# Layer boundary of a two-layer streaming encoder step: the second normalisation from three sums gathered in the projection, six channel units over k-tiles, adaLN block 6 between them, and the first adaLN loads behind a gate

## The chip, the core and the metric

One core of a Trainium2 chip runs the whole program in one launch. The metric is device time of an execution in microseconds (us): the median of the runs, and beside it one execution taken with the hardware profiler, whose span is read below. The engines are called by their names in the profile: PE (TensorE, matmuls; PEld are its weight loads), DVE (VectorE), ACT (ScalarE), POOL (GpSimd) and SP (SyncE, which issues most loads).

## What is computed

320 tokens (256 of a prompt, 64 of a sample) of width 2048 pass two layers. Layer 0 mixes a state-space part and sliding-window attention, layer 1 is a gated short convolution. Around each mixer stands the same frame, and the change lies where the frame of layer 0 ends and that of layer 1 begins:

```python
def rms_norm(x, w):
    y = x * lax.rsqrt(jnp.mean(x * x, axis=-1, keepdims=True) + EPS)
    return y * w
def modulate(x, c, w_ada, b_ada, g_pre):
    mod = jax.nn.silu(c) @ w_ada + b_ada             # adaLN
    shift, scale, gate = jnp.split(mod[:, None, :], 3, axis=-1)
    return rms_norm(x, g_pre) * (1 + scale) + shift, gate
for layer in range(DEPTH):                           # 2 layers, prompt and sample alike
    h, gate = modulate(x, c, w_ada[layer], b_ada[layer], norm_pre[layer])
    o = mixer(h)                                     # ends with "@ w_out"; layer 1 begins with "h @ w_in"
    x = x + gate * rms_norm(o, norm_post[layer])
```

So x1 = x + r0 * t, where t is layer 0's output o times its gate and norm weight, and r0 = rsqrt(mean(o^2) + EPS) is one number per token. Layer 1 needs r1 = rsqrt(mean(x1^2) + EPS). Since r0 does not depend on the channel, mean(x1^2) = mean(x^2) + 2 r0 mean(x t) + r0^2 mean(t^2).

## The kernel before

All activations lie transposed in SBUF: 128 channels on the partitions by 320 tokens, 16 such tiles ("n" or "kt", 0 to 15) for the width 2048, four to a buffer of a pool called act. A product takes fp32 weights and activations that are split in two parts each, so that one 128x128 by 128x320 product is three matmuls (high by high, high by low, low by high). `block` loads 1 MB of weights by SP, splits each half of it (`split`: ACT writes the high part of 128x1024, DVE subtracts to get the low part) and queues the half's 24 matmuls; queued halves ("jobs") run two later, and between them `tick` advances side work.

The names that matter here:

- The projection of layer 0 ends in eight calls of `pair` (m = 0 to 7), each for two tiles n of the output. Their PSUM tiles are "pot", the weights' parts "wot". After the last matmul of tile n `close` runs: DVE adds the PSUM to the tile o, ACT squares it (fq), DVE adds the square to facc, ACT multiplies the tile by its gate.
- adaLN comes in blocks of 512 columns; block b's four quarters (`ada_pe`, sub = 0 to 3) are 16 small matmuls each. Quarters of block 5 and the first of block 6 stand between the pairs, seven more (6,1 to 7,3) in the boundary (`more`); their weights "adaw" are loaded by SP. At the same time `ada_side` works block 4 of layer 1 on DVE (adac, two 128x512 products per step of a load "adas"), at a rate per tick.
- The boundary follows: `by_token` sums facc over the partitions (three 128x1 matmuls), `rstd` makes r0 from it on 128x3 elements and spreads it to all partitions by three matmuls (rp0b). `residual` then takes each tile: DVE multiplies o by r0, DVE (even n) or POOL (odd n) adds x and writes x1 (`x<-xr,o`), ACT squares it (x1q), and PE adds the square into x1s by an fp32 matmul with ones. From x1s come r1t, r1 and r1b in the same way, and `modulate` makes layer 1's input, hh and hl, tile by tile.
- Layer 1's first channel block c = 0 has four units n (u, gc, g, gb), worked over k-tiles: `wc_block(j)` for j = 0 to 3 takes k-tiles 4j to 4j+3 for all four units (PSUM tiles "c"), so that PE can start when the first tiles of hh are there. The blocks c = 1 to 31 take one unit after the other over all 16 k-tiles (PSUM tiles "pc").
- At the start of the program `ada_fetch(2)` has POOL issue four loads "adaw" of 512 KB for blocks that PE takes up later, while SP loads x, the adaLN weights w0[0] to w0[7] of the first two tiles ("w" in the profile, PE's "adaf") and the first weights of the mixer ("early", "ahead").

The order of most instructions is decided when the program is built, by a scheduler that goes by its own costs; where `pin[0]` is set, PE and SP keep the order of the code. DVE, ACT and POOL each run their instructions strictly in the order that results.

## Time and profile before

| | us |
|---|---|
| median of 3 runs (lowest, highest) | 2163.41 (2160.16, 2163.43) |
| the profiled execution, whole time | 2157.34 |
| its span, which the views divide | 2155.6 |
| PE busy in the span | 2125.1 (99%) |
| DVE busy | 1403.8 (65%) |
| ACT busy | 898.5 (42%) |
| POOL busy | 188.2 (9%) |

In the profiled execution layer 0's last projection ends at about 980 us, and layer 1's channel blocks run from 1005 us on. Times in the views are microseconds from the start of the span. "start, us" rows give a begin and a duration; "x32" is a count of instructions; "<-" in a name reads "written from"; "[... <-DMA adaw]" is idle time of the engine ahead of the row and what ended it. Matmuls are pipelined, so that one shows about 0.31 us but the next starts 0.15 us after it.

### The profile page before, as it was taken

How to read it: one execution, taken by the hardware profiler on the slowest of the kernel's cores; microseconds unless marked ns; L12 is line 12 of the kernel's file. 1: busy time of each engine (PE TensorE's matmuls, PEld its weight loads, DVE VectorE, ACT ScalarE, POOL GpSimd, SP SyncE). 2: the span in 40 equal slices, each digit the busy share in tenths (PEclk: the TensorE clock that was granted, in tenths of full speed). 3: DMA queues.
4: the chain of work that ended last, by engine and by line, in shares of the span. 5: the costliest groups of instructions: out<-in, count | busy, mean ns of one | idle time of the engine just before them, and what ended most of it. 6: DMA issues, size and time to landing. Idle time of an engine off the chain costs nothing.

```text
span 2155.6 us, 38215 instructions
## 1 busy us (share of the span) xinstructions
PE 2125.1 (99%) x15659; PEld 2065.6 (96%) x15659; DVE 1403.8 (65%) x2273; ACT 898.5 (42%) x1473; POOL 188.2 (9%) x433
## 2 busy tenths in 40 slices
...
GB/s 340 388 287 176 168 161 185 157 262 188 172 184 205 173 181 213 272 267 233 172 176 169 159 176 159 178 172 177 155 164 169 163 163 174 171 137 157 150 145 88
DMA packets 88767, 408.82 MB, mean 190 GB/s; under 512 B 10992, under 2 KB 11920, under 8 KB 52496
## 3 DMA queue, kind: packets, MB, share of 16 engines
...
q8 instruction: 122, 2.00, 0.4%
q14 instruction: 53, 0.43, 0.1%
...
## 4 chain that ended last, share of the span: by engine, by line
PE 58%; DVE 1%; issue 1%; DMA 0%; POOL 0%; ACT 0%; POOLq 0%; ACTq 0%; DVEq 0%
PE pc L47 41%; PE poe L47 5%; PE pod L47 5%; PE pot L47 3%; PE c L47 1%; PE pos L47 1%; PE adap L47 1%; DVE adac L285 1%; PE pb L47 0%; PE x1s L47 0%; DMA adaw<-in_wada 0%; DVE wot0l L174 0%; DVE wos7l L174 0%; DVE o L1173 0%; PE st L47 0%
## 5 line engine op out<-in xcount | busy, mean ns | idle before, releaser
L285 DVE SCALAR_TENSOR_TENSOR adac<-adas,cs,adac 128x512 f32<-128x512 f32 x420 | 300.4, 746 | 60.0 <-DMA adas<-in_wada 60.0
L1241 POOL COPY ncc<-cp 128x2 f32<-128x2 f32 x32 | 6.0, 186 | 940.5 <-DVE cp L1239 940.5
L47 PE MATMUL adap<-adaw,cs 128*32 128x128 f32 x1152 | 37.8, 277 | 2.8 <-DMA adaw<-in_wada 2.7
L956 POOL COPY nca<-xp 128x3 f32<-128x3 f32 x24 | 23.0, 958 | 196.2 <-ACT xp L954 196.2
L47 PEld LDWEIGHTS adap<-adaw,cs 128*32 128x32 f32 x1152 | 30.9, 111 | 7.7 <-issue 4.1
L762 ACT ACTIVATE pr<-s,mx 128x192 f32<-128x192 f32 (+2 forms) x80 | 29.8, 406 | 14.9 <-DVE mx L757 14.9
L1246 DVE SCALAR_TENSOR_TENSOR cc<-cp,ccw,cc 128x322 f32<-128x322 f32 x64 | 35.3, 552 | 1.1
L541 POOL DMA_DIRECT2D adaw<-in_wada x48 | 25.2, 530 | 91.7 <-PE adap L47 48.8
L1239 DVE TENSOR_TENSOR cp<-pc,u 128x256 f32<-128x256 f32 x31 | 13.2, 425 | 30.3 <-PE pc L47 30.2
L990 ACT ACTIVATE sg<-sg,acum 128x128 f32<-128x128 f32 (+1 forms) x96 | 29.3, 376 | 8.4 <-POOL sg L982 8.3
L1254 DVE TENSOR_TENSOR sgg<-pc,sgg 128x320 f32<-128x320 f32 x31 | 15.2, 490 | 19.0 <-PE pc L47 18.9
L961 DVE SCALAR_TENSOR_TENSOR cv<-xp,convaw,cv 128x323 f32<-128x323 f32 x48 | 26.5, 552 | 0.7
L982 POOL TENSOR_SCALAR_AFFINE_SELECT sg<-sg 128x512 f32<-128x512 f32 (+1 forms) x24 | 21.9, 920 | 38.5 <-DMA sg<-acs_b 38.4
L598 DVE TENSOR_TENSOR q<-s,q 128x320 f32<-128x320 f32 x32 | 15.0, 489 | 15.0 <-PE s L47 15.0
L1160 DVE TENSOR_TENSOR oo<-poe,oo 128x320 f32<-128x320 f32 x16 | 7.9, 492 | 25.6 <-PE poe L47 25.6
L47 PE MATMUL s<-hh,ws_0h 128*128 128x320 f32 x64 | 20.2, 315 | 1.2 <-ACT ws_1h L170 1.2
L47 PE MATMUL s<-hl,ws_0h 128*128 128x320 f32 x64 | 19.9, 311 | 1.5 <-DVE hl L493 1.5
L47 PE MATMUL s<-hh,ws_1h 128*128 128x320 f32 x64 | 20.5, 320 | 0.0
L47 PE MATMUL s<-hh,ws_2h 128*128 128x320 f32 x64 | 20.4, 319 | 0.0
L47 PE MATMUL s<-hh,ws_2l 128*128 128x320 f32 x64 | 19.8, 309 | 0.0
L47 PE MATMUL s<-hh,ws_1l 128*128 128x320 f32 x64 | 19.8, 309 | 0.0
L47 PE MATMUL s<-hh,ws_0l 128*128 128x320 f32 x64 | 19.8, 309 | 0.0
...
## 6 DMA issues: line engine op xcount, KB each, us to landing
...
adaw<-in_wada POOLq DMA_DIRECT2D x48, 512.0 KB, 9.5
...
```

The source lines that it names most:

```text
L47: ins = f(*a, **k)
L285: V.scalar_tensor_tensor(acc[s], w, c, acc[s], op0=ALU.mult, op1=ALU.add)
L541: G.dma_start(t[m], i["wada"][q[0], q[1], q[2]][:, 2 * m : 2 * m + 2, :])
L598: V.tensor_tensor(dst, ps, a, op=ALU.add)
L762: S.activation(pr[m][u // 2][:, u % 2, a : a + CH[c][2]], ss[m][u // 2][:, u % 2, a : a + CH[c][2]], AF.Exp, bias=mx[:, j, u : u + 1], sca ...
L956: G.tensor_copy(nca[:, ci, 0, :], xp[:, 256:259])
L961: V.scalar_tensor_tensor(cv, xp[:, n : n + 323], cw[:, ci, n : n + 1], cv, op0=ALU.mult, op1=ALU.add)
L982: G.affine_select(sg, sg, pattern=[[0, 4], [1, nt]], base=0, channel_multiplier=-1, compare_op=ALU.is_ge, fill=NEG)
L990: S.activation(sgs[b][n][:, h, :], sgs[b][n][:, h, :], AF.Exp, bias=acum[0:nt, b, hd : hd + 1])
L1239: V.tensor_tensor(xp[:, 2:258], ps[:, 0:256], u[:, 0:256], op=ALU.mult)
L1246: V.scalar_tensor_tensor(cv, xp[:, m : m + 322], ccw[:, c, m : m + 1], cv, op0=ALU.mult, op1=ALU.add)
L1254: V.tensor_tensor(sg, ps, sg, op=ALU.mult)
```

## The change

Five things are changed at once.

1. In the projection `close` does more for each tile: ACT also squares the gated tile (tq), DVE adds that square to tacc[0], POOL multiplies x by the tile (tx) and adds the product to tacc[1]. The last tile's three squares and products stay apart (last_sq), and its product is DVE's.
2. In the boundary the mean of x1's squares is put together on 128x3 elements from sums over the partitions of facc, tacc[0], tacc[1] (p9) and of the last tile's three (q9), r0, and the saved mean square of x (vxx). `residual`, the 16 squares x1q and the matmuls x1s go. `root` and `spread` are the two halves of `rstd`.
3. The first k-tile stage takes six units, the four of c = 0 and the first two of c = 1, four k-tiles at a time. Its first weights (wj) are loaded and split ahead of the boundary. x1 and hh, hl are made in this stage, tile by tile, x1 three tiles ahead (`x1_tile`, `h_tile`); POOL does 14 of the 16 adds to x1.
4. Block 6's four quarters stand in the boundary, with weights loaded ahead (two by POOL into act buffers, two by SP in eight pieces adaz); block 7's stand in the k-tile stage. Blocks 8 to 11 on DVE begin after c = 1 and no longer before c = 0.
5. At the start the first four adaLN loads of POOL wait for w0[7] to land. POOL also copies vxx there.

The core of the diff (ada_turn's and the removed parts' lines are cut):

```diff
     def rstd(ps, n, name, table=False, base=None):
...
+        if name == "r0":
+            G.tensor_copy(vxx, v)
...
-    ada_fetch(2)
+    landed = wk.tile([128, 1], F32, tag="rt", name="landed")
+    behind = G.tensor_copy(landed, w0[7][:, 3, 0:1])
+    with tc.issue_after(behind.ins):
+        ada_fetch(2)
...
     def close(n, l, ps):
...
         for s, a, b in SEGS:
             S.activation(t[:, a:b], t[:, a:b], AF.Identity, scale=mod[l][:, 2, n, s : s + 1])
+        if l == 0:
+            x = xr[n // 4][:, n % 4, :]
+            if n < KT - 1:
+                sumsq(tacc[0], t, n == 0, f"tq{n}")
+                c = tacc[1] if n == 0 else stile([128, T], f"tx{n}")
+                G.tensor_tensor(c, x, t, op=ALU.mult)
+                if n:
+                    G.tensor_tensor(tacc[1], tacc[1], c, op=ALU.add)
+            else:
+                last_sq.extend([stile([128, T], f"tq{n}"), stile([128, T], f"tx{n}")])
+                S.activation(last_sq[1], t, AF.Square)
+                V.tensor_tensor(last_sq[2], x, t, op=ALU.mult)
...
     for m in range(8):
         pair(i["wos"][1, m], f"ot{m}", ys, 8, ...)
-        if m in (0, 1, 2, 4, 6):
+        if m in (0, 1, 2, 4):
             ada_pe(*later.pop(0), make=mmps, end=True)
+        if m == 5:
+            first += later
+            ada_fetch(2)
     finish_side()
...
+    wj = wp.tile([128, 16, 128], F32, tag="w", name="wj")
+    nc.sync.dma_start(wj, i["wc"][0])
+    ab = [halves(wj[:, 0:8, :], "wja"), halves(wj[:, 8:16, :], "wjb")]
     flush()
+    pin[0] = True
...
+    for m, a in enumerate((facc, tacc[0], tacc[1])):
+        sums9(p9, m, a)
...
+    sums9(q9, 0, last_sq[0])
+    quarter()
+    sums9(q9, 1, last_sq[1])
+    sums9(q9, 2, last_sq[2])
...
+    y0 = root(w9[:, 0:3], "rp0")
+    quarter()
+    pb0 = spread(y0, "rp0")
+    wt, wx = w9[:, 3:6], w9[:, 6:9]
+    V.scalar_tensor_tensor(wt, q9[:, 3:6], 1.0 / D, b9[:, 3:6], op0=ALU.mult, op1=ALU.add)
+    V.scalar_tensor_tensor(wx, q9[:, 6:9], 2.0 / D, b9[:, 6:9], op0=ALU.mult, op1=ALU.add)
+    V.tensor_tensor(wt, wt, y0, op=ALU.mult)
+    V.tensor_tensor(wt, wt, wx, op=ALU.add)
+    V.tensor_tensor(wt, wt, y0, op=ALU.mult)
+    V.tensor_tensor(wt, wt, vxx, op=ALU.add)
+    V.tensor_scalar(wt, wt, EPS, None, op0=ALU.max)
+    y1 = root(wt, "r1")
+    quarter()
+    row6 = ada_row(1, 6, quarter())
+    ada_turn(1, 6, row6)
...
+    def x1_tile(n, rs):
+        t, to, x = ot[n // 4][:, n % 4, :], x1[n // 4][:, n % 4, :], xr[n // 4][:, n % 4, :]
+        V.tensor_tensor(t, t, rs, op=ALU.mult)
+        (V if n < 2 else G).tensor_tensor(to, x, t, op=ALU.add)
+    def h_tile(n, rs):
...
+        V.tensor_tensor(xn, x1[g][:, k, :], rs, op=ALU.mult)
...
+            S.activation(hi, xn[:, c], AF.Identity, scale=sc, bias=sh)
...
+                S.activation(t[:, c], hi.bitcast(F32), AF.Identity, scale=-1.0, bias=sh)
...
+                V.scalar_tensor_tensor(lo, xn[:, c], sc, t[:, c], op0=ALU.mult, op1=ALU.add)
+    x1_tile(0, pb0)
+    S.activation(rs0, pb0, AF.Copy)
+    for n in range(1, 4):
+        x1_tile(n, rs0)
+    pb1 = spread(y1, "r1")
+    h_tile(0, pb1)
+    S.activation(rs1, pb1, AF.Copy)
+    for n in range(1, 4):
+        x1_tile(n + 3, rs0)
+        h_tile(n, rs1)
+    ada_fetch(2)
...
         if c == 0:
+            jobs.append(joint)
+            c1_block(0)
             for j in range(1, 4):
-                wc_block(j)
-                modulate(x1, rs, 1, 4 * j, 4, h1)
+                for m in range(2):
+                    for n in (4 * j + 2 * m, 4 * j + 2 * m + 1):
+                        if n + 3 < KT:
+                            x1_tile(n + 3, rs0)
+                        h_tile(n, rs1)
+                    if m == 0:
+                        wc_block(j)
+                    else:
+                        c1_block(j)
+                    if j == 1:
+                        quarter()
+                        ada_fetch(2)
+                    elif j == 2:
+                        got = quarter()
...
```

The order of instructions at three places follows; the numbers in names are the buffers'. First PE at the boundary. Before, from the last matmul of the projection to the first sums of squares, quarters of adaLN (adap) lie around the sums of facc (rp0t) and the spread of r0 (rp0b):

```order
L47 MATMUL pot_11168<-ysh_10343,wot7l_11097 128x320
L47 MATMUL adap_11027<-adaw_6_1_11218,cs 32x128 x16
L47 MATMUL adap_11027<-adaw_6_2_11240,cs 32x128 x5
L47 MATMUL rp0t<-ones,facc_9502 128x1 x3
L47 MATMUL adap_11027<-adaw_6_2_11240,cs 32x128 x11
L47 MATMUL adap_11027<-adaw_6_3_11258,cs 32x128 x16
L47 MATMUL rp0b<-rp0d,ones 128x128 x2
L47 MATMUL rp0b<-rp0d,ones 128x64
L47 MATMUL adap_11276<-adaw_7_0_11277,cs 32x128 x16
L47 MATMUL x1s<-x1q_11316,ones 128x320
L47 MATMUL x1s<-x1q_11321,ones 128x320
```

Now, on the same engine from the same place, where rp and rq are p9 and q9, and the last of the three rp waits for POOL's sum tacc[1]:

```order
L47 MATMUL pot_11277<-ysh_10347,wot7l_11168 128x320
L47 MATMUL rp_11311<-ones,facc_9506 128x1 x3
L47 MATMUL rp_11311<-ones,tacc_10363 128x1 x3
L47 MATMUL rp_11311<-ones,tacc_10364 128x1 x3
L47 MATMUL rq_11312<-ones,fq_11303 128x1 x3
L47 MATMUL adap_6_11329<-adaw_00_11011,cs 32x128 x8
L47 MATMUL adap_6_11329<-adaw_01_11012,cs 32x128 x8
L47 MATMUL rq_11312<-ones,tq_11307 128x1 x3
L47 MATMUL rq_11312<-ones,tx_11308 128x1 x3
L47 MATMUL adap_6_11329<-adaw_10_11015,cs 32x128 x8
L47 MATMUL adap_6_11329<-adaw_11_11016,cs 32x128 x8
L47 MATMUL rp0b<-rp0d,ones 128x128 x2
```

The sums of squares over 16 tiles are gone from PE, 18 sums of one column stand in their place, and from the last rp on every matmul waits in line behind them. Second DVE in the middle of the projection. Before, between one tile's add of PSUM (L1160) and the second next:

```order
L1160 TENSOR_TENSOR o_5157<-pot_10614,o_5157 128x320
L285 SCALAR_TENSOR_TENSOR adac_4_0_10588<-adas_4_2_10477,cs,adac_4_0_10588 128x512
L385 TENSOR_TENSOR facc_9502<-facc_9502,fq_10644 128x320
L285 SCALAR_TENSOR_TENSOR adac_4_1_10589<-adas_4_2_10477,cs,adac_4_1_10589 128x512
L174 TENSOR_TENSOR wot3l_10674<-wot_10671,wot3h_10673 128x1024
L285 SCALAR_TENSOR_TENSOR adac_4_0_10588<-adas_4_3_10586,cs,adac_4_0_10588 128x512
L285 SCALAR_TENSOR_TENSOR adac_4_1_10589<-adas_4_3_10586,cs,adac_4_1_10589 128x512
L1160 TENSOR_TENSOR o_5439<-pot_10677,o_5439 128x320
L285 SCALAR_TENSOR_TENSOR adac_4_0_10588<-adas_4_4_10627,cs,adac_4_0_10588 128x512
L385 TENSOR_TENSOR facc_9502<-facc_9502,fq_10707 128x320
L174 TENSOR_TENSOR wot3l_10713<-wot_10671,wot3h_10712 128x1024
```

Now, over the same kind of stretch a little later:

```order
L1166 TENSOR_TENSOR o_5443<-pot_10750,o_5443 128x320
L286 SCALAR_TENSOR_TENSOR adac_4_0_10604<-adas_4_5_10677,cs,adac_4_0_10604 128x512
L286 SCALAR_TENSOR_TENSOR adac_4_1_10605<-adas_4_5_10677,cs,adac_4_1_10605 128x512
L175 TENSOR_TENSOR wot4l_10798<-wot_10795,wot4h_10797 128x1024
L388 TENSOR_TENSOR facc_9506<-facc_9506,fq_10780 128x320
L388 TENSOR_TENSOR tacc_10363<-tacc_10363,tq_10785 128x320
L286 SCALAR_TENSOR_TENSOR adac_4_0_10604<-adas_4_6_10718,cs,adac_4_0_10604 128x512
L286 SCALAR_TENSOR_TENSOR adac_4_1_10605<-adas_4_6_10718,cs,adac_4_1_10605 128x512
L1166 TENSOR_TENSOR o_5443<-pot_10801,o_5443 128x320
L175 TENSOR_TENSOR wot4l_10843<-wot_10795,wot4h_10842 128x1024
```

Each tile's group has one add more (tacc), and the adac steps have stayed. Third POOL, before the projection's end. Before, its instructions from the loads of xr on, with no arithmetic until the adds of x1 in the boundary:

```order
L1183 DMA xr_10353<-in_xT 128x1280
L1183 DMA xr_10354<-in_xT 128x1280
L88 DMA ccw<-in_convcw 128x96
L88 DMA cprevc<-in_cprevc 128x64
L1222 TENSOR_TENSOR x_0_11208<-xr_10351,o_5157 128x320 x2
L1222 TENSOR_TENSOR x_1_11209<-xr_10352,o_5439 128x320 x2
```

Now, from the same loads on, the first of 29 operations that run beside the projection:

```order
L1202 DMA xr_10358<-in_xT 128x1280
L544 DMA adaw_00_11011<-in_wada 128x1024
L544 DMA adaw_01_11012<-in_wada 128x1024
L544 DMA adaw_10_11015<-in_wada 128x1024
L1182 TENSOR_TENSOR tacc_10364<-xr_10355,o_5161 128x320
L544 DMA adaw_11_11016<-in_wada 128x1024
L1182 TENSOR_TENSOR tx_10558<-xr_10355,o_5161 128x320
L1184 TENSOR_TENSOR tacc_10364<-tacc_10364,tx_10558 128x320
L1182 TENSOR_TENSOR tx_10629<-xr_10355,o_5161 128x320
L1184 TENSOR_TENSOR tacc_10364<-tacc_10364,tx_10629 128x320
```

POOL has moved from idle to two operations for each tile of the projection.

More of the change, by code (lines that the diff above doesn't have):

```diff
@@ L304, in ada_row, with ada_turn @@
         return row
[L306 to L307 removed]
+    def ada_turn(l, b, row, one=None, pool=None):
+        pt = pool.tile([128, 128], F32, tag="ada", name=f"adat{l}_{b}") if pool else sps([128, 128], f"adat{l}_{b}_{one}")
         if one is None:
@@ new lines, in spread @@
+    def spread(y, name):
+        dg = wk.tile([128, 3, 128], F32, tag="dg", name=name + "d", bufs=1)
+        pb = sps([128, T], name + "b")
+        for b, (t0, c0, n_) in enumerate(TB):
+            V.tensor_scalar(dg[:, b, :], ident, y[:, b : b + 1], None, op0=ALU.mult)
+            PE.matmul(pb[:, t0 + c0 : t0 + c0 + n_], lhsT=ones, rhs=dg[:, b, c0 : c0 + n_], start=True, stop=True)
+        return pb
+    w9 = wk.tile([128, 9], F32, tag="w9", name="w9", bufs=1)
+    V.scalar_tensor_tensor(w9[:, 0:3], q9[:, 0:3], 1.0 / D, b9[:, 0:3], op0=ALU.mult, op1=ALU.add)
@@ L1257, in hybrid_stream_step @@
     h1 = ([], [])
-    p4 = [once(f"c0{n}", mmps if n < 2 else lambda name: sps([128, T], name)) for n in range(4)]
-    def wc_block(j):
-        en = []
-        for n in range(4):
-            en += [(p4[n], 4 * j + k, j == 0 and k == 0, j == 3 and k == 3,
-                    (lambda ps, n=n: channels(0, n, ps)) if j == 3 and k == 3 else None) for k in range(4)]
-        block(i["wc"][j], f"wc{j}", en, h1)
-    pq = mmps("x1s")
-    def square(n, t):
-        sq = stile([128, T], f"x1q{n}")
-        S.activation(sq, t, AF.Square)
-        PE.matmul(pq, lhsT=ones, rhs=sq, start=n == 0, stop=n == KT - 1)
@@ L1274, in more @@
-    def more(n=1):
-        for _ in range(n):
-            if later:
-                ada_pe(*later.pop(0), make=mmps, end=False)
-    more(1)
-    residual(0, xr, square, [V, G] * 8)
-    wc_block(0)
-    row = stile([1, T], "x1row")
-    V.tensor_copy(row, pq[0:1, :])
-    sums = by_token(row, "r1t", ones[0:1, 0:1])
-    more(3)
-    rs = rstd(sums, D, "r1", True)
-    assert not later
-    for b in (6, 7):
-        ada_end(1, b, ada_ps[b])
-    modulate(x1, rs, 1, 0, 4, h1)
-    side["gen"] = ada_side([(1, b) for b in range(8, 12)])
@@ L1294, in hybrid_stream_step, with entries6 @@
-    side["rate"] = RATE_D
+    p6 = [once(f"c{n // 4}{n % 4}", mmps if n in (0, 1, 4) else lambda name: sps([128, T], name)) for n in range(6)]
+    def entries6(j, units):
+        return [(p6[n], 4 * j + k, j == 0 and k == 0, j == 3 and k == 3,
+                 (lambda ps, n=n: channels(n // 4, n % 4, ps)) if j == 3 and k == 3 else None)
+                for n in units for k in range(4)]
+    KMAJOR = [0, 4, 1, 5, 2, 6, 3, 7]
+    def wc_block(j):
+        block(i["wc"][j], f"wc{j}", entries6(j, range(4)), h1, order=KMAJOR)
```

108 lines of the change are left out of this document (81 added, 27 removed).

## Prediction

> **What bounds the kernel now.** I read the page first, then the chain of waits around 980 us, then the busy time by stretch, then the queues of DVE and POOL where work is added. From the page (engine, busy us, share of the span, instructions):
>
> ```profile
> span 2155.6 us, 38215 instructions
> PE 2125.1 (99%) x15659; PEld 2065.6 (96%) x15659; DVE 1403.8 (65%) x2273; ACT 898.5 (42%) x1473; POOL 188.2 (9%) x433
> ```
>
> PE is the bound over the whole, so time can come only from PE work that goes or from PE's waits, and both lie thick at the boundary. The chain there (start, us, what):
>
> ```profile
> 979.71 1.05 PE adap L47 x32
> ...
> 980.78 6.55 DMA adaw<-in_wada
> ...
> 989.03 6.64 PE x1s L47 x20
> ...
> 996.01 3.43 PE x1s L47 x12
> 999.44 1.01 PE adap L47 x32
> ...
> 1001.24 0.17 DVE r1v L345
> ...
> 1002.48 0.30 DVE r1d L363
> ...
> 1003.80 0.49 DVE mt L397
> ...
> 1005.11 0.95 PE c L47 x3
> ...
> 1007.97 18.05 PE c L47 x123
> ...
> 1035.79 4.25 PE pc L47 x29
> ```
>
> The projection ends at 979.71, the first c matmul starts at 1005.11, and the units of c = 0 are done when pc (PSUM of the next units) begins at 1035.79. A c matmul takes 18.05/123 = 0.147 us, an adaLN quarter 1.01 us. The stretches (us, then PE, PEld, DVE, ACT, POOL busy, granted clock, DMA share, GB/s):
>
> ```profile
> 12.00:32.00 20.00, 15.17 (x113) 12.81 (x113) 10.12 (x31) 6.18 (x14) 1.06 (x2) 0.59 1.03 409
> 930.00:970.70 40.70, 40.70 (x360) 38.73 (x359) 40.67 (x63) 22.68 (x42) 0.00 (x0) 1.00 0.79 273
> 970.70:980.20 9.50, 9.50 (x81) 9.30 (x85) 3.18 (x9) 5.30 (x12) 0.00 (x0) 1.00 0.44 154
> 1005.10:1035.80 30.70, 30.32 (x227) 29.40 (x228) 29.42 (x77) 19.73 (x41) 0.65 (x4) 1.00 0.59 210
> ```
>
> In the projection from 930 to 970.7 us DVE is busy 40.67 of 40.70 us, although PE is what waits for nothing there: DVE is full at the place where the change adds to it. Only the last 9.5 us give it 6.3 us of air.
>
> **Boundary and k-tiles.** Before, the stretch 979.71 to 1035.79 is 56.1 us. The same work that the change puts there includes 96 matmuls of c = 1, which before run later as pc (96 x 0.147 = 14.1), and the quarter 6,0, which before stands in the projection (1.01): 71.2 us to compare with.
>
> After, PE's path to the first c matmul has two roots in a row. The rows of before for the first one (DVE; the two of ACT are one tile's square and gate in the projection):
>
> ```profile
> 979.75 0.49 DVE L1160 TENSOR_TENSOR o<-pot,o 128x320 f32<-128x320 f32 x1 [2.00 <-PE pot L47]
> 982.19 0.16 DVE L345 TENSOR_SCALAR rp0v<-rp0t 128x3 f32<-128x3 f32 x1 [0.92 <-PE rp0t L47]
> 984.68 0.89 DVE L1217 TENSOR_TENSOR o<-o,rp0b 128x320 f32<-128x320 f32 x2 [0.58 <-PE rp0b L47]
> 957.20 0.47 ACT L381 ACTIVATE fq<-o 128x320 f32<-128x320 f32 x1
> 957.71 0.75 ACT L1169 ACTIVATE o<-o,mod 128x256 f32<-128x256 f32 x2
> ```
>
> From the last pot matmul to the use of rp0b that is 4.97 us. The change lengthens it: q9 needs the last tile's o, its square, its gate, the gated tile's square and its product with x (0.49, then 0.47 + 0.75 + 0.47 on ACT, with the 0.49 of the product beside the last), a quarter (1.01) stands between the sums and pushes them, and three b9 operations of about 0.2 come before the root: I take 3.0 more, so rp0b at 8.0. Then seven operations on 128x3 (0.2 each: six steps fill 1001.24 to 1002.48, ACT's root among them) of which five lie behind rp0b, 1.0; the root, the same 1.2; the spread, from r1d to mt, 1.3, during which DVE works at its first x1 tiles (two multiplies in 0.89) and is 1.2 late for the next step; then mt, hh to c, 1003.80 to 1005.11, 1.3. Sum 14.0, with a lower bound of 9.3 (4.97 + 1.2 + 1.3 + 1.3 + 0.5, all extra work beside the quarters). Three of the four quarters in the boundary stand in this idle time and cost nothing; the fourth delays q9 and is in the 3.0. Behind it: 288 c matmuls x 0.147 = 42.2, four quarters of block 7, 4.1. PE's wait for adaw, which ends the DMA row at 980.78, goes, since block 6's weights are fetched during the projection. In the k-tile stage each group of four k-tiles is 72 matmuls, 10.6 us of PE, against DVE's 4 x (0.44 for the multiply of x1, 0.44 for xn and, as an estimate, 0.55 for lo's two pieces) + 3 splits of 1.18 (a row below) = 9.3: near the bound, but under it; with POOL's four adds beside it I take 3 us of stalls for the stage, and 1 for the late DVE at adap below. After: 14.0 + 42.2 + 4.1 + 4.0 = 64.3. **Term 1: -6.9 us** (-11.6 at the lower bound, -2 with stalls of 8).
>
> The 16 squares x1q on ACT become 16 tq, earlier; the 32 x1s passes, 6.64 + 3.43 us on PE, go, and 18 one-column sums of 128 rows come, which is in the 14.0. wj's two splits move from the boundary ahead of it, into DVE's air after 970.7. The eight SP loads adaz stand in SP's queue among the wot loads: the DMA share is 0.79 there, so they are hidden; the four POOL loads stand ahead of POOL's first products. Blocks 8 to 11 begin some 20 us later on DVE, which is idle half the time of c = 1 on (the page's 65%): nothing. One small buffer less (spo, 11 to 10): nothing.
>
> **The sums in the projection.** Added: 14 adds and a copy on DVE, 16 squares on ACT, 29 products and adds of 128x320 on POOL. The groups on DVE from 930 to 970.7 us (count, busy, mean ns):
>
> ```profile
> L285 DVE SCALAR_TENSOR_TENSOR adac<-adas,cs,adac 128x512 f32<-128x512 f32 x30 | 21.6, 744 | 0.0
> L385 DVE TENSOR_TENSOR facc<-facc,fq 128x320 f32<-128x320 f32 x10 | 4.9, 485 | 0.0
> L1160 DVE TENSOR_TENSOR o<-pot,o 128x320 f32<-128x320 f32 x10 | 4.8, 484 | 0.0
> ```
>
> Ten more adds put DVE 4 to 5 us late at 970.7 (485 ns each, stepping at 0.44 as the two multiplies above). The place where PE first asks for it is the end of block 4, adap from adac:
>
> ```profile
> 967.79 1.41 DVE L285 SCALAR_TENSOR_TENSOR adac<-adas,cs,adac 128x512 f32<-128x512 f32 x2
> 969.36 0.43 PE L47 MATMUL adap<-adac,es 128*32 128x128 f32 x8
> ```
>
> adac ends at 969.20 and PE starts on it at 969.36, with no slack; in the changed order some 17 matmuls more of the projection stand ahead of it, 2.5 us, so DVE's 4 us cost about 1.5 (the 1 counted above, the rest in term 2). ACT is busy 22.68 of 40.7 and takes 0.47 x 10 more: hidden.
>
> Then POOL. It has no arithmetic in the projection before, so its price beside a full DVE is read elsewhere (POOL and DVE):
>
> ```profile
> 985.65 8.25 POOL L1222 TENSOR_TENSOR x<-xr,o 128x320 f32<-128x320 f32 x7 [2.67 <-DVE o L1217]
> 994.10 3.25 POOL L1222 TENSOR_TENSOR x<-xr,o 128x320 f32<-128x320 f32 x1 [0.19 <-DVE o L1217]
> 994.27 2.35 DVE L174 TENSOR_TENSOR wc0l<-wc,wc0h 128x1024 fp32r<-128x1024 f32 x2
> 864.13 4.92 POOL L982 TENSOR_SCALAR_AFFINE_SELECT sg<-sg 64x256 f32<-64x256 f32 x2 [3.77 <-DMA sg<-acs_b]
> 681.26 1.12 DVE L1002 TENSOR_TENSOR xw<-xd,te 128x512 f32<-128x512 f32 x1
> 864.33 0.67 DVE L1002 TENSOR_TENSOR xw<-xd,te 64x512 f32<-64x512 f32 x1
> L1353 POOL TENSOR_TENSOR x<-x,oo 128x320 f32<-128x320 f32 x6 | 5.0, 856 | 130.6 <-DVE oo L1351 130.6
> ```
>
> The last row is the price of such a POOL operation alone, 0.86 us. Seven adds of x1 on POOL step at 8.25/7 = 1.18 us beside DVE's o multiplies, which read PSUM; the eighth stands beside two weight splits that read SBUF twice, and takes 3.25: 2.35 of waiting and about 0.9 of work. So a POOL operation and a DVE operation with two inputs in SBUF do not run together; mostly POOL waits, and now and then DVE does (xw 1.12 us with a POOL select beside it; 0.67 for the shape with half the rows without). [...]
>
> Bounds: nothing at all, if POOL fits beside the o adds and into DVE's gaps; against it, 29 x 0.86 = 24.9 us of POOL work, less what is free of DVE's two-input work: the 6.3 us of air in the last stretch minus 4 tacc adds (4.6 left) 16 o adds of 0.44 (7.0) and, as an estimate from the share of 40.67 in 40.70, nothing before it: 13.3 us; without the o adds 20.3. What makes POOL's lag felt is the ring of small buffers: fq and tq of a tile reuse buffers that POOL's adds three tiles back must have left, so ACT, and behind it the weight splits and PE, wait when POOL is more than about three tiles late; and PE's rp waits for the last tacc[1]. I take half of the 13.3, rounded down to 6 us, because the nearest rows, the same operation of the same shape, cost DVE nothing (seven at 1.18, with DVE's cadence unbroken), while the eighth shows that beside splits POOL gets through only once in 3 us, where the projection asks for two in 3.9. **Term 2: +6 us** (0 to +20.3).
>
> **The gate at the start.** The waits of PE up to 46 us, its first product of the mixer, POOL's first loads, the loads by size, and PE's use of them (last times: first and last start):
>
> ```profile
> PE warm L47 <- DMA x<-in_xT: 4.1, 1, 4.1
> PE adaf L47 <- DMA w<-in_wada: 2.0, 2, 1.1
> 28.35 0.64 PE L47 MATMUL sa<-hh,wsa0h 128*128 128x320 f32 x1 [1.54 <-ACT hh L479]
> 3.78 2.12 POOL L541 DMA_DIRECT2D adaw<-in_wada  x4
> adaw<-in_wada POOLq DMA_DIRECT2D x12, 512.0 KB, 9.1
> L47 PEld LDWEIGHTS adap<-adaw,cs x128: 106/110/110, 43.7 to 52.2; 128*32 128x32 f32 x128
> ```
>
> The DMA engines are full from 12 to 32 us (share 1.03 at 409 GB/s, above), PE waits for x and w, and four loads of 0.52 MB each, 2.1 MB, that nobody needs then are issued at 3.78 ahead of most of them: 2.1 MB at 409 GB/s is 5.1 us of stream. Moved behind w0[7], they let x, w and the first weights land up to 5.1 us sooner. Part is lost where the next things decide (PE's first sa waits for hh at 28.35 already, and the granted clock is 0.59 there). Against: w0[7] lands, as I estimate from the stream, near 25 us; the four then land 9 us later, and PE reads them at 43.7 us before, some 40 after: in time by about 5 us. vxx's copy on POOL waits for r0v, which is earlier than w0[7]. **Term 3: -3.5 us** (-5.1 to +1, if the late loads hold up the weights that follow).
>
> **Sum.** -6.9 + 6 - 3.5 = -4.4 us. The profiled execution was 2157.34 us (span 2155.6 and 1.7 around it): 2152.9 by its scale. The median of the runs is 6.1 above that execution, so I predict 2159.0 for the median. Within 0.2%, 4.3 us, a measurement of this kernel can hardly tell from no change; the forecast lies at that edge. Its own range is -8 to -1: 2155 to 2162.
>
> **Rivals.** A, POOL is hidden: the waiting operations cost DVE nothing, as in the seven adds, and only terms 1 and 3 count: -10.4, 2153. For it speaks that POOL mostly is the one that waits and may lie three tiles behind; against it the 3.25 us. Chance 0.19.
>
> B, POOL starves in the projection: DVE's gapless queue leaves it no turn (the 64x256 select at 864.13 shows 4.92 us for two, with DVE busy throughout), the ring stops ACT, DVE gets gaps only by PE standing still, and POOL's 24.9 us less the 4.6 at the end and 2 of the o adds are paid, 18.3: -6.9 + 18.3 - 3.5 = +7.9, 2171.3. [...] Against it: the o adds and ACT's slack. Chance 0.26, of which a third stays within 4.3 us.
>
> C, the k-tile stage turns DVE-bound: DVE's 9.3 x 4 and POOL's 14 adds of 0.86 come to 49 us there, if they exclude each other, against 46.3 of PE: stalls of 10 instead of 3, +2.6, 2166. For it: DVE was busy 29.42 of 30.70 in this stage already. Chance 0.08.
>
> D, the gate gives nothing: another load or the chain from w to the first hh takes the place of the wait: -0.9 or a little above, 2162 to 2165. Chance 0.11.
>
> The forecast has 0.36, of it half over 0.2% faster. Faster: 0.18 + 0.19 + 0.04 = 0.41; slower: B 0.17, C 0.05, D 0.04 = 0.26; the same 0.33. The range for 8 in 10 goes from A with the short boundary (-10.4 - 4.7, 2148) to B (2171); B's upper bound of 20.3 and a gate that backfires lie outside.
>
> **What would show it.** Right: no row DMA adaw and no x1s in the boundary; first c matmul 12 to 16 us after the last pot; tx and tacc operations of POOL at 1 to 3 us each; adac or o of DVE at up to 1.5 us now and then; the last pot matmul less than 9 us late against the start's gain; first sa at about 25 us and not 28. Wrong: PE waits for ACT or POOL of over 10 us in the projection (B), or none and POOL at 0.86 (A); c waiting for hl in every group (C); sa at 28 still (D).

## The result, and the profile after

The changed kernel takes 2188.64 us (median of 4 runs, 2186.94 to 2189.16) against 2162.81 us of the kernel before in the same set: ratio 1.013, 95% interval 1.0117 to 1.0142. It is 26 us slower, where 4 us less was forecast. Its profiled execution took 2186.94 us, with a span of 2185.2, 29.6 us more than the span before; that is more than 26 because the profiled execution of before lies 5.5 us below the median of its set, and that of the changed kernel 1.7. The page's first lines:

```profile
span 2185.2 us, 38354 instructions
PE 2133.7 (98%) x15651; PEld 2073.5 (95%) x15651; DVE 1433.0 (66%) x2276; ACT 910.4 (42%) x1505; POOL 239.3 (11%) x482
```

PE has the same work and stands still longer. Where, is read from the begin and end of PE's groups, to about 0.1 us ("pot" is the projection, "c" the k-tile stage, "sa" and "s" the first products of the mixer). The rows e1 to e12 are the experiments of the next section; the stage c has four units in before and in the kernels made from it (e4, e5, e8, e10, e11), and six in the others:

| kernel | first sa | first s | first pot | pot, first to last | last pot to first c | c, first to last |
|---|---|---|---|---|---|---|
| before | 28.4 | 59.8 | 912.5 | 67.2 | 25.4 | 30.7 |
| changed | 19.4 | 56.2 | 912.0 | 83.2 | 25.0 | 59.2 |
| e1, no POOL sums | 19.4 | 55.9 | 911.3 | 69.5 | 22.0 | 59.2 |
| e2, x1 on DVE | 20.6 | 54.7 | 908.7 | 84.4 | 24.6 | 52.0 |
| e3, PE kept busy | 19.4 | 55.7 | 912.3 | 83.0 | 21.8 | 59.2 |
| e4, before with the gate | 20.6 | 54.7 | 909.9 | 67.2 | 25.5 | 30.7 |
| e5, before with POOL's sums | 28.4 | 60.8 | 917.6 | 80.7 | 25.1 | 32.2 |
| e6, all sums on DVE | 20.6 | 54.3 | 910.7 | 83.6 | 23.3 | 52.0 |
| e7, e1 + e2 + e3 | 21.2 | 56.8 | 914.3 | 70.7 | 21.5 | 52.0 |
| e8, e4 and early weights | 19.6 | 58.0 | 914.5 | 67.3 | 27.0 | 32.1 |
| e9, e7 with quarters first | 19.9 | 53.9 | 909.6 | 71.0 | 22.9 | 48.1 |
| e10, e4 with the gate at w0[3] | 19.9 | 56.5 | 911.4 | 67.3 | 24.9 | 30.7 |
| e11, e4 once more | 19.6 | 55.2 | 910.1 | 67.3 | 24.8 | 32.2 |
| e12, e9 without matmuls before c | 19.3 | 56.8 | 914.0 | 71.5 | 21.0 | 50.3 |

In the forecast's terms: the start, -0.5 at the first pot; the projection, 83.2 for 66.2 (67.2 less the quarter 6,0), +17.0; boundary and k-tiles, 25.0 + 59.2 = 84.2 for 71.2, +13.0. Sum +29.5, the difference of the spans.

The stretches of the changed kernel (columns as in the prediction):

```profile
930.00:970.70 40.70, 34.48 (x268) 32.79 (x268) 40.15 (x53) 20.81 (x40) 18.96 (x16) 0.96 0.61 213
970.70:995.20 24.50, 17.28 (x118) 14.94 (x116) 24.15 (x31) 13.13 (x26) 12.12 (x10) 1.00 0.61 202
995.20:1020.20 25.00, 17.03 (x179) 15.22 (x178) 14.09 (x47) 6.01 (x17) 5.82 (x8) 0.66 0.09 29
1020.20:1079.40 59.20, 53.97 (x419) 50.62 (x420) 46.77 (x83) 38.27 (x80) 19.69 (x26) 0.88 0.53 180
```

In the projection DVE is full as before but gets through 53 instructions in 40.7 us, where it got through 63 before, and PE is down to 34.48 of 40.70. The groups on DVE from 925 to 996 us, then POOL's from 905 to 1080 us:

```profile
L286 DVE SCALAR_TENSOR_TENSOR adac<-adas,cs,adac 128x512 f32<-128x512 f32 x30 | 26.2, 894 | 0.0
L388 DVE TENSOR_TENSOR tacc<-tacc,tq 128x320 f32<-128x320 f32 x12 | 12.2, 1014 | 0.3 <-ACT tq L384 0.3
L388 DVE TENSOR_TENSOR facc<-facc,fq 128x320 f32<-128x320 f32 x13 | 8.3, 639 | 0.5 <-ACT fq L384 0.5
L1166 DVE TENSOR_TENSOR o<-pot,o 128x320 f32<-128x320 f32 x13 | 6.2, 479 | 1.2 <-PE pot L47 1.2
L284 DVE TENSOR_SCALAR adac<-adas,cs 128x512 f32<-128x512 f32 x2 | 1.6, 791 | 0.0
```

```profile
L1182 POOL TENSOR_TENSOR tx<-xr,o 128x320 f32<-128x320 f32 x14 | 17.4, 1241 | 39.8 <-ACT o L1175 33.5 <-DVE adac L286 5.4 <-DVE adac L284 0.8
L1369 POOL TENSOR_TENSOR x<-xr,o 128x320 f32<-128x320 f32 x14 | 16.6, 1193 | 7.2 <-DVE o L1368 7.2
```

Against before, adac goes from 744 to 894 ns and the add facc from 485 to 639; tacc, the same operation as facc, takes 1014. The add o, one of whose inputs is in PSUM, stays at 479 for 484. So what POOL's operations hold here are the adds and products of DVE that read SBUF twice, and not the add that reads PSUM. The last row, two operations with one such input and a scalar per partition, goes from 480 to 791, so that an operation can be held without two full inputs in SBUF. A mean hides two cases: of the 13 facc adds ten take 0.47 to 0.49 us and three 1.16 to 1.17. POOL itself waits little, 1.24 us for 0.86 alone, and stands idle most of the time. What PE waited for from 900 to 1080 us, the longest sums:

```profile
PE pot L47 <- DVE o L1166: 6.4, 4, 3.0
PE pot L47 <- DVE wot6l L175: 5.2, 2, 2.9
PE rp L47 <- DVE facc L388: 3.9, 1, 3.9
PE c L47 <- ACT hh L1381: 3.8, 2, 3.6
PE c L47 <- DVE hl L1391: 3.4, 3, 1.7
```

And PE at the boundary, in order of time:

```profile
994.93 0.31 PE L47 MATMUL pot<-ysh,wot7l 128*128 128x320 f32 x1
999.12 1.44 PE L47 MATMUL rp<-ones,facc 128*128 128x1 f32 x6 [3.88 <-DVE facc L388]
1000.66 2.72 PE L47 MATMUL rp<-ones,tacc 128*128 128x1 f32 x12
1003.24 1.42 PE L47 MATMUL rq<-ones,fq 128*128 128x1 f32 x6
1004.59 1.93 PE L47 MATMUL adap<-adaw,cs 128*32 128x128 f32 x32
1006.46 1.44 PE L47 MATMUL rq<-ones,tq 128*128 128x1 f32 x6
1007.76 1.42 PE L47 MATMUL rq<-ones,tx 128*128 128x1 f32 x6
1009.11 1.93 PE L47 MATMUL adap<-adaw,cs 128*32 128x128 f32 x32
1010.97 1.54 PE L47 MATMUL rp0b<-rp0d,ones 128*128 128x128 f32 x6
1012.44 2.80 PE L47 MATMUL adap<-adaz,cs 128*32 128x128 f32 x64
1015.81 0.79 PE L47 MATMUL r1b<-r1d,ones 128*128 128x128 f32 x6
1020.18 0.42 PE L47 MATMUL c<-hh,wjah 128*128 128x320 f32 x1 [3.58 <-ACT hh L1381]
```

From 999 to 1015 us PE is hardly ever idle: the sums and adaLN quarters themselves are the path. 18 sums of one column take 7.9 us, a quarter 1.9 for 1.01 before. The granted clock, the column ahead of the DMA share, says why they are slow:

```profile
995.00:1000.00 5.00, 1.12 (x7) 0.88 (x5) 4.07 (x8) 2.69 (x7) 1.60 (x3) 0.72 0.34 118
1000.00:1005.00 5.00, 4.90 (x29) 4.79 (x33) 1.30 (x5) 1.40 (x4) 1.24 (x2) 0.50 0.03 10
1005.00:1010.00 5.00, 5.00 (x64) 4.42 (x57) 0.75 (x6) 0.20 (x1) 0.00 (x0) 0.50 0.02 3
1010.00:1015.00 5.00, 5.00 (x90) 4.30 (x82) 3.52 (x20) 0.21 (x1) 0.00 (x0) 0.58 0.00 0
1020.00:1030.00 10.00, 7.55 (x25) 6.52 (x25) 10.00 (x17) 5.26 (x13) 8.89 (x10) 0.55 0.58 193
1030.00:1040.00 10.00, 9.51 (x67) 9.32 (x71) 10.00 (x17) 5.89 (x13) 7.98 (x9) 0.77 0.67 233
```

It falls to 0.50 in PE's gap of 3.9 us (it is 1.00 from 995 to 997 us and 0.54 from 997 to 999), is back at about 1014, and falls again at about 1021, behind the gap of 3.6 us ahead of c. In the k-tile stage, from 1020 to 1040, DVE is busy 20 of 20 us.

### The profile page after: what moved, and what is told of

Same layout as the page of the kernel before. It is cut to its first block, busy times and chain, and to the rows that moved or that the text cites. A ratio compares the mean times of both kernels' runs of the same rounds, so it can differ in the third digit from the quotient of the medians.

```text
span 2185.2 us, 38354 instructions
## 1 busy us (share of the span) xinstructions
PE 2133.7 (98%) x15651; PEld 2073.5 (95%) x15651; DVE 1433.0 (66%) x2276; ACT 910.4 (42%) x1505; POOL 239.3 (11%) x482
## 4 chain that ended last, share of the span: by engine, by line
PE 54%; DVE 4%; issue 1%; DMA 1%; ACT 1%; POOL 0%; SPq 0%; ACTq 0%; DVEq 0%; POOLq 0%
PE pc L47 39%; PE pod L47 5%; PE poe L47 5%; PE c L47 1%; DVE adac L286 1%; PE pos L47 1%; DMA adas<-in_wada 1%; PE adap L47 1%; DVE tacc L388 1%; DMA adaw<-in_wada 1%; PE pb L47 0%; PE pot L47 0%; DVE facc L388 0%; DVE hl L1391 0%; DVE o L1368 0%
## 5 line engine op out<-in xcount | busy, mean ns | idle before, releaser
L286 DVE SCALAR_TENSOR_TENSOR adac<-adas,cs,adac 128x512 f32<-128x512 f32 x420 | 305.2, 755 | 79.2 <-DMA adas<-in_wada 79.1
L544 POOL DMA_DIRECT2D adaw<-in_wada x60 | 31.7, 532 | 74.1 <-PE adap L47 42.8
L47 PEld LDWEIGHTS adap<-adaw,cs 128*32 128x32 f32 x1088 | 29.5, 113 | 10.7 <-DMA adaw<-in_wada 5.2
L996 ACT ACTIVATE sg<-sg,acum 128x128 f32<-128x128 f32 (+1 forms) x96 | 29.5, 375 | 10.2 <-POOL sg L988 10.2
L1315 DVE TENSOR_TENSOR cp<-pc,u 128x256 f32<-128x256 f32 x30 | 12.7, 423 | 25.1 <-PE pc L47 25.1
L1182 POOL TENSOR_TENSOR tx<-xr,o 128x320 f32<-128x320 f32 x14 | 17.4, 1241 | 39.8 <-ACT o L1175 33.5
L47 PE MATMUL s<-hl,ws_0h 128*128 128x320 f32 x64 | 19.9, 311 | 1.7 <-DVE hl L496 1.7
L1381 ACT ACTIVATE hh<-xn,mod 128x256 fp32r<-128x256 f32 (+1 forms) x32 | 15.1, 512 | 15.1 <-DVE xn L1377 13.7
```

The costliest lines, as they stand in the source:

```text
L47: ins = f(*a, **k)
L286: V.scalar_tensor_tensor(acc[s], w, c, acc[s], op0=ALU.mult, op1=ALU.add)
L544: G.dma_start(t[m], i["wada"][q[0], q[1], q[2]][:, 2 * m : 2 * m + 2, :])
L996: S.activation(sgs[b][n][:, h, :], sgs[b][n][:, h, :], AF.Exp, bias=acum[0:nt, b, hd : hd + 1])
L1182: G.tensor_tensor(c, x, t, op=ALU.mult)
```

## The experiments

The theory after this reading has three parts: POOL's operations hold DVE in the projection (L), its adds of x1 hold DVE in the k-tile stage (K), and PE's small matmuls at half clock make the boundary long (C). Against L stands that DVE's own new adds are the cause; against C, that DVE and ACT are the path and the clock only follows. The median of before in the sets of the experiments is 2159.5 to 2160.2 us.

**e1, no POOL sums** (changed kernel):

```diff
-                c = tacc[1] if n == 0 else stile([128, T], f"tx{n}")
-                G.tensor_tensor(c, x, t, op=ALU.mult)
-                if n:
-                    G.tensor_tensor(tacc[1], tacc[1], c, op=ALU.add)
+                if n == 0:
+                    G.tensor_tensor(tacc[1], x, t, op=ALU.mult)
```

> The changed kernel without POOL's work beside the projection: the 28 products and adds of tiles 1 to 14 (tx, tacc[1]) are left out, so mean(x t) has only two tiles in it; all else stays. Theory L (POOL and DVE exclude each other, and POOL's operations stretch DVE's: in the changed kernel adac takes 894 ns for 745, tacc 1014 for 485): the projection, first to last pot matmul, falls from 83.2 us to about 70 (67.2 before, less the quarter 6,0, plus some 4 for the tacc adds), and the whole by 12 to 18 us, the more if PE's gap ahead of the sums rp gets so short that the clock holds. Rival: the tacc adds on DVE alone are what DVE cannot take; then the projection stays at 79 or more and the whole gains under 4 us.

Measured 2170.19 us (ratio to before 1.0045, interval 1.003 to 1.006), 18 less than the changed kernel. The projection is 69.5 us, 13.7 less. On DVE from 925 to 982 us:

```profile
L286 DVE SCALAR_TENSOR_TENSOR adac<-adas,cs,adac 128x512 f32<-128x512 f32 x30 | 21.8, 751 | 0.0
L388 DVE TENSOR_TENSOR tacc<-tacc,tq 128x320 f32<-128x320 f32 x13 | 6.4, 491 | 0.5 <-ACT tq L384 0.4
```

The tacc adds are all there and take 491 ns each; the projection is only 3.3 us above the 66.2. L holds and its rival falls: the adds that DVE got cost 3 us, POOL's work 14.

**e2, x1 on DVE** (changed kernel):

```diff
-        (V if n < 2 else G).tensor_tensor(to, x, t, op=ALU.add)
+        V.tensor_tensor(to, x, t, op=ALU.add)
```

> The changed kernel with all 16 adds of x1 on DVE, none on POOL. Theory K (in the k-tile stage POOL's adds hold DVE up: xn and o take 1.07 to 1.15 us beside them for 0.48 alone, and DVE is busy 10.00 of 10.00 us from 1020 to 1040): DVE gets 14 x 0.40 = 5.6 us more work and loses about 9 of stretching, so the stage, first to last c matmul, falls from 59.2 to about 55, the whole by 3 to 6 us. Rival: DVE is simply full there and the stage gets 5 us longer.

Measured 2178.82 us (1.0085, 1.0067 to 1.0103), 10 less than the changed kernel. The stage falls by 7.2 us although DVE does 14 adds more. The multiply of x1 on DVE, of the changed kernel and then here, from 1017 us on:

```profile
L1368 DVE TENSOR_TENSOR o<-o,rs 128x320 f32<-128x320 f32 x14 | 8.9, 661 | 0.0
```

```profile
L1368 DVE TENSOR_TENSOR o<-o,rs 128x320 f32<-128x320 f32 x12 | 5.6, 495 | 0.0
```

Here the r0 that it multiplies by lies in SBUF (rs0); in the kernel before it lay in PSUM, and the same multiply ran beside POOL's adds without loss (482 ns in the mean). K holds.

**e3, PE kept busy** (changed kernel; `keep(n)` runs n fp32 matmuls of 128x320 into a PSUM tile that nobody reads):

```diff
+    keep(6)
     p9, q9 = sps([128, 9], "rp9"), sps([128, 9], "rq9")
...
     pb1 = spread(y1, "r1")
+    keep(5)
```

> The changed kernel with 6 extra fp32 matmuls of 128x320 on PE between the last pot and the first rp, and 5 between r1b and the first c, about 0.6 us each, into a PSUM tile that nobody reads. In the changed kernel PE stands still for 3.9 and 3.6 us there, and after each gap the granted clock is 0.50 for 17 and 14 us. Theory C (the clock falls because PE stood still, and PE's small matmuls are on the path): the clock stays at 1, the sums and quarters from 999 to 1014 take half as long (7 us less) and the first c matmuls 4 to 6 us less: the whole falls by 7 to 13 us. Rival: the path there is DVE's and ACT's, the clock only follows; then nothing changes, or it gets 1 us slower.

Measured 2184.29 us (1.0114, 1.0097 to 1.013), 4 less than the changed kernel: less than expected. The boundary is 3.2 us shorter, the stage the same to 0.1 us. The granted clock:

```profile
1000.00:1002.00 2.00, 1.29 (x12) 1.27 (x12) 0.67 (x1) 1.46 (x4) 1.31 (x2) 1.00 0.06 22
1002.00:1004.00 2.00, 2.00 (x42) 1.69 (x41) 0.69 (x4) 0.00 (x0) 0.00 (x0) 0.93 0.04 8
1004.00:1006.00 2.00, 2.00 (x14) 2.00 (x10) 0.00 (x0) 0.00 (x0) 0.00 (x0) 0.50 0.00 0
1006.00:1010.00 4.00, 4.00 (x46) 3.38 (x47) 2.17 (x14) 0.20 (x1) 0.00 (x0) 0.50 0.00 0
```

The clock holds through the gap, and falls at 1004 all the same, with no gap of PE over 0.71 us, behind twelve sums of one column and a quarter (999.2 to 1004.0). In the k-tile stage the clock held until 1024 and no time came of it: there C's rival is right, DVE is the path (busy 2.00 of every 2.00 us from 1014 to 1036).

**e4 and e11, the gate alone** (kernel before):

```diff
-    ada_fetch(2)
+    landed = wk.tile([128, 1], F32, tag="rt", name="landed")
+    behind = G.tensor_copy(landed, w0[7][:, 3, 0:1])
+    with tc.issue_after(behind.ins):
+        ada_fetch(2)
```

> The kernel before with the gate at the start alone (POOL's first four adaLN loads wait for w0[7]). In the changed kernel the first sa matmul came 9.0 us sooner, of which 3.4 were left at 60 us and up to 856 us. Theory: these 3.4 us stay to the end, since PE is the bound: 2159.4, and 2162 if 2.7 of them are lost again at 860 us as in the changed kernel. Rival: all of it is paid back, within 1 us of before.

> The kernel before with the gate at w0[7] once more, on the same chip as the gate at w0[3] and with more rounds: if the 3.3 us (ratio 0.9987, interval 0.9974 to 1.0) are the gate's, 0.998 to 0.9995 again, with the interval clear of 1.

Measured 2156.91 (0.9987, 0.9974 to 1.0) and 2156.62 us (0.9984, 0.9976 to 0.9993): 3.3 and 3.5 us faster than before, a version that beats both. In these two and in the changed kernel the first sa comes 7.8 to 9.0 us sooner, and at the first s 3.6 to 5.1 us are left. The changed kernel at its start, PE's wait and the two stretches in which the gain goes:

```profile
PE adap L47 <- DMA adaw<-in_wada: 3.1, 1, 3.1
```

```profile
40.00:50.00 10.00, 6.80 (x90) 5.83 (x89) 4.40 (x10) 1.89 (x4) 1.58 (x3) 0.91 1.01 413
50.00:60.00 10.00, 8.85 (x72) 8.43 (x74) 9.28 (x21) 5.04 (x10) 1.05 (x2) 0.92 1.04 417
```

The DMA queues are full until 60 us (share 1.01 and 1.04); what was put off is missing there.

**e10, the gate at w0[3]**: `w0[3]` in place of `w0[7]` in the lines above.

> The kernel before with the gate alone, but behind w0[3] and not w0[7], so that POOL's loads are issued some 8 us sooner. With the gate at w0[7] the first sa came 7.8 us sooner and 5.1 were left at 60 us, since the DMA queues are full from 40 to 60 us (share 1.02) and PE waits 1.7 us for the late adaLN weights. Theory: the bytes up to 60 us bound the start; the first sa then comes some 5 us sooner, less is paid back, and the whole is the same as with the gate at w0[7], 2156 to 2158. Rival: w0[4] to w0[7] and the first weights get late again and the gain falls under 2 us.

Measured 2157.81 us (0.9992, 0.9983 to 1.0001). The first sa came at 19.9, 8.4 us sooner where 5 were expected. Then PE waited 3.4 us for adar, a copy by ACT that stands behind a split of mixer weights for which ACT waited 4.2 us (`ahead`, by DMA), and 3.3 us were left at the first s. So some first weights got late, as the rival has it, and 2.3 us were gained in all. That the bytes up to 60 us bound the gain fits; whether w0[3] or w0[7] is better is not told apart by 1 us.

**e5, POOL's sums alone** (kernel before):

```diff
             S.activation(t[:, a:b], t[:, a:b], AF.Identity, scale=mod[l][:, 2, n, s : s + 1])
+        if l == 0 and n < KT - 1:
+            c = cross if n == 0 else stile([128, T], f"tx{n}")
+            G.tensor_tensor(c, xr[n // 4][:, n % 4, :], t, op=ALU.mult)
+            if n:
+                G.tensor_tensor(cross, cross, c, op=ALU.add)
```

> The kernel before with POOL's 29 products and adds of x and the gated tiles beside the projection, as the changed kernel has them, and nothing else of the change; the sum they form is not used. Theory L: DVE is full from 930 to 970 us, and each POOL operation of about 0.86 us that gets in holds a DVE operation with two SBUF inputs: the projection (67.2 us) gets 8 to 13 longer, adac's mean rises from 745 to 850 or more, the whole is 8 to 14 us slower than before. Rival: POOL only waits, DVE is not held; then within 2 us of before.

Measured 2175.75 us (1.0069, 1.0052 to 1.0086), 16 slower than before and 2 above the expected range. The projection is 80.7 us for 67.2, +13.5; over it DVE is busy 73.3 us for 59.6, 13.7 more, with 101 instructions in both kernels. On DVE from 925 to 992 us, and POOL's group:

```profile
L285 DVE SCALAR_TENSOR_TENSOR adac<-adas,cs,adac 128x512 f32<-128x512 f32 x32 | 29.4, 949 | 0.0
L385 DVE TENSOR_TENSOR facc<-facc,fq 128x320 f32<-128x320 f32 x12 | 9.3, 774 | 0.7 <-ACT fq L381 0.7
```

```profile
L1172 POOL TENSOR_TENSOR tx<-xr,o 128x320 f32<-128x320 f32 x14 | 17.7, 1262 | 32.4 <-ACT o L1169 25.4 <-DVE adac L285 7.0
```

adac 949 ns for 744, facc 774 for 485: POOL alone does it, with nothing else of the change there. Here too an operation is held or not: of these adac, twenty take 0.73 to 0.75 us and most of the others 1.34 to 1.40.

**e6, all sums on DVE**: the changed kernel with `V` for `G` in the products and adds of e1 and in the line of e2.

> The changed kernel with all of POOL's arithmetic on DVE, the 29 products and adds of the projection and the adds of x1; the computation is whole. By theory L, DVE is no longer stretched (16 us in the changed kernel's projection) but has 11.6 us more to do (29 x 0.40): the projection goes from 83.2 to about 79, the k-tile stage from 59.2 to 52 as with x1 on DVE alone, the whole 9 to 13 us faster than the changed kernel, near 2177. Rival: POOL at least works beside DVE for part of the time, and the projection gets longer than 83.

Measured 2177.2 us (1.0077, 1.0064 to 1.009), as expected for the whole; the stage is 52.0, but the projection 83.6 and not 79. DVE does the 29 operations itself at 0.40 and more a step, and loses as much as when POOL held it. Here, where DVE is full, the sums cost 14 us on either engine.

**e7, the three together** (e1, e2 and e3 in one).

> The changed kernel with all three suspected costs taken out at once: POOL's 28 products and adds of the projection left out (the sum of x t is not whole), the adds of x1 on DVE, and the extra matmuls in PE's two gaps. If the three account for the loss, their gains add up: 18 + 10 + 4 = 32 us less than the changed kernel, 2156; that would be no faster than before with the gate alone (2157), so that the rebuilt boundary itself is worth nothing on this chip. If the forecast's term of -6.9 us for the boundary holds once the lock and the clock are out of the way, 2150.

Measured 2162.44 us (1.0011, 1.0002 to 1.002). 26 us less than the changed kernel, not 32: in e1 alone the shorter gap had already given the boundary 3.0, which e3's 3.2 give once; the other 3 are not accounted for. Last pot to last c is 73.5 us: with POOL's hold on DVE and the first gap out of the way still not the 64.3 of the forecast.

**e8, gate and early weights** (kernel before with the gate; the quarter 7,0's weights by SP in four pieces to small buffers):

```diff
+                if q[1:] == (7, 0):
+                    raw = [stile([128, 512], f"adaz{k}") for k in range(4)]
+                    for k in range(4):
+                        nc.sync.dma_start(raw[k], i["wada"][q[0], q[1], q[2]][:, k, :])
...
```

> A version that may beat both: the kernel before with the gate at the start, and with the weights of the quarter 7,0 loaded by SP in four pieces to small buffers ahead, so that PE need not wait 2.7 us for them at 984.7 and its clock need not fall (0.50 to 0.71 from 988 to 992 in before). Expected: 3 us from the gate as in the kernel with the gate alone, 2.7 from the wait and about 1.5 from the clock, 2153 to 2156. Rival: the chain there is DVE's (o, x1) and PE's squares only come later: no more than the gate's 3 us.

Measured 2161.2 us (1.0002, 0.9993 to 1.001): no gain, and of the gate's gain only 1.8 us were left at the first s. The loads were not early: SP issued them from 983.5 on, and PE waited longer than before (2.7):

```profile
L1285 SPq DMA_DIRECT2D adaz<-in_wada x4: 425/429/889, 983.5 to 985.4; - x4
```

```profile
PE adap L47 <- DMA adaz<-in_wada: 3.4, 1, 3.4
```

It does not test what it was made for.

**e9, quarters first, and e12, without the matmuls before c** (e7 with block 6's quarters ahead of the sums; e12 without `keep(5)`):

```diff
-    keep(6)
+    for _ in range(3):
+        quarter()
+    row6 = ada_row(1, 6, quarter())
+    keep(2)
     p9, q9 = sps([128, 9], "rp9"), sps([128, 9], "rq9")
...
```

> As the kernel with no POOL sums, x1's adds on DVE and PE kept busy (2162.4; last pot to first c 21.5 us), but block 6's four quarters run right behind the last pot matmul, in PE's first gap, in place of four of the extra matmuls there, and no longer between the sums and the roots (28 of the products and adds of x t are left out here too). Theory: the quarters lay on the path, two of them at half clock (1.2 and 1.9 us, then 2.2 for two), and cost 3 to 4 us there that the forecast had put at nothing: last pot to first c 17 to 18.5 us, the whole 3 to 4 us faster, 2159. If the clock falls all the same because sums of one column do not count as work, the sums stay at 0.24 us and more each and the gain is at the lower end. Rival: they were hidden beside DVE's roots: 21 us as before.

> The kernel with block 6's quarters first (2158.9; last pot to last c 71.0 us: 22.9 and 48.1), without the five extra matmuls between r1b and the first c, since there they ended the chain (5.35 us at half clock ahead of the first c; 28 of the products and adds of x t are left out here too). If those matmuls only stood in the way: first c 2 us sooner, the stage the same, last pot to last c 68 to 69 us, 2157. If they paid by bringing the clock back (0.58 in 1001 to 1004, 1.0 behind): the stage gets as much longer as the first c comes sooner, 71 us again. In neither case the 64.3 us of the forecast.

Measured 2158.89 (0.9994, 0.9985 to 1.0003) and 2161.46 us (1.0001, 0.999 to 1.0011). Their profiled executions differ by 5.2 us, of which 4.4 are there at the first pot already, ahead of what differs. rp0b starts 10.4 us after the last pot in e9 and 11.8 in e12, for 12.0 in e7 and 15.7 in the changed kernel. Up to there e9 and e12 do the same, and both begin the sums 4.7 us after the last pot; what parts them is the clock, which in e9 fell behind the 18 sums (they took 3.9 us) and in e12 among them (5.4). So moving the quarters gained 0.2 to 1.6 us, and not the 3 to 4 expected: ahead of the sums they put these off by 1.7 us against e7, and at their old places PE now waits for DVE's two roots, 1.6 us for rp0d and 4.35 for r1d in both runs. That the quarters had been on the path is not shown. e9's first c came 22.9 us after the last pot, later than the 17 to 18.5 expected, since the extra matmuls ended the chain (5.35 us at a clock of 0.50 to 0.58); e12 shows that these neither cost nor gained: first c 1.9 us sooner, the stage 2.2 longer, 71.3 for 71.0. The clock and PE in e12:

```profile
990.00:995.00 5.00, 5.00 (x36) 4.92 (x34) 0.30 (x3) 0.00 (x0) 0.00 (x0) 0.77 0.00 0
995.00:1000.00 5.00, 2.41 (x11) 2.03 (x10) 2.92 (x18) 0.72 (x4) 3.70 (x8) 0.50 0.27 66
```

```profile
990.21 0.72 PE L47 MATMUL rp<-ones,facc 128*128 128x1 f32 x6
994.24 1.42 PE L47 MATMUL rq<-ones,tx 128*128 128x1 f32 x6
```

PE is busy 5.00 of 5.00 us, from 990.2 on with sums of one column, at full clock at the start (0.72 for three) and at half at the end (1.42). 71 us is what the same work took before. So with the sums of x t for nothing, which no kernel has, the rebuilt boundary gains nothing.

## Why the prediction was wrong

The sum was -4.4 us and the spans differ by +29.6. Term by term:

- **Term 3, the gate, -3.5.** Right in size: -3.6 at the first s, and -3.3 and -3.5 us for the gate alone. The way there was another, so that the size is partly luck: the gain at the first sa is 9.0 us, more than the 5.1 that I had as its upper bound, and then over half is paid back, because the put-off 2.1 MB are missing while the queues are full up to 60 us. At the first pot 2.3 to 2.6 us were left in e4 and e11 and 0.5 in the changed kernel, but single executions do not settle so little: e5, which has no gate, came there at 917.6 us, 5.1 later than before. Part of this is the granted clock, which fell to 0.50 for 3.4 to 6.8 us around 865 us in most executions and not in those of before, e2 and e9. Why it did is not shown.
- **Term 2, the sums, +6 (0 to 20.3).** It is +17.0, of which 13.5 are POOL's (e5) and 3.3 DVE's adds (e1). The upper bound worked out in the text, 13.3, was the measured price to 0.2 us, which is luck in part, since it has 0.86 us for a POOL operation and those took 1.2; the step that failed is the choice of half of it. I had taken the seven adds that cost DVE nothing as the nearest row. They stood beside multiplies with r0 in PSUM, which kept their 482 ns; the projection has adac, facc and weight splits, and e5 shows these held: 949 ns for 744 and 774 for 485 in the mean, and 1.55 and 1.57 us for 1.22 in the splits of wot7 and wot6. The row to take was xw, held from 0.67 to 1.12 us. (The row of 0.67 that I gave as one without POOL lies within POOL's two selects of 864.13; there POOL was held, one select for 4.55 us against a median of 0.64 on that line, and not DVE.) I priced rival B near enough, 18.3, but told it wrongly: POOL did not starve behind DVE, its operations took 0.4 us longer than alone, and DVE stood.
- **Term 1, boundary and k-tiles, -6.9.** It is +13.0, and this is the step that failed by most, 20 us. The stage: 59.2 us against the 50.3 of the sum. The 3 us of stalls, and 1 for DVE's lateness, were 12.9, and 7.2 of it are POOL's adds of x1 (e2). Rival C had the stalls at 10, with a chance of 0.08; but the 49 us of DVE and POOL against 46.3 of PE beside it give about 3 and not 10, so that it came near is luck. The boundary: 25.0 against 14.0. The first use of rp0b, 8.0 us after the last pot in the sum, came 17.4 after it (1012.62), which is 9.4 of the 11.0. Of these the 18 one-column sums are 7.9. The sum says of them "which is in the 14.0", but no term of the 14.0 has a price for them, although a row in the chain of before shows three of them:

```profile
1000.45 0.77 PE r1t L47 x6
```

  That is 4.6 us for 18; it was 3.9 in e9 with the clock at 1, and 7.9 here. The quarter among them took 1.9 us for 1.0. That the other three "stand in this idle time and cost nothing" is about right: the next takes 1.9 us where e9 and e12 wait 1.6 for rp0d, and from rp0b to the first c it is 9.2 us here with the last two and 9.3 in e12 without them. And the granted clock was not in the sum. The rows of before showed it, 0.59 at the start, and 0.93 in the boundary's stretch:

```profile
980.20:1005.10 24.90, 20.06 (x237) 14.69 (x229) 17.39 (x53) 11.20 (x27) 11.77 (x10) 0.93 0.74 263
```

  That gaps matter is seen in e3, where the filled gap kept the clock at 1.00 up to 1002 us, for 0.50 to 0.54 from 997 on in the changed kernel. How long a gap it takes is not shown: the clock fell 2 us into the gap of 3.9, fell in before between 986 and 988 us behind a wait of 2.7, and fell in e3 and e12 with no gap over 0.71. Nor is it shown what brings the clock back: 15 us of sums and quarters without a gap (999 to 1014 us) stayed at 0.50.
- **The cases.** Rivals B and C were set against each other, with their chances added up, and both came true in the same run: both are DVE held by POOL, at two places (13.5 us in e5, 7.2 in e2). Had they been one case, the range would have reached to 2178 by the prices given, still 10 us short, about what the boundary's 11 are.

The lower bound of the boundary, 9.3 us, was never near: 21.0 is the least that any of the kernels had. The rebuilt boundary trades 16 wide sums on PE (32 passes, 10 us, beside which DVE did its work in any case) for 18 small sums and two roots with little between them.
